# A streaming encoder layer: head norm's inverse root on one engine, the residual scaled before it is spilled, caches loaded earlier

## The chip, the cores and the metric

The kernel runs on one core of a Trainium2 chip. The core has a matrix engine (TensorE, PE in the profile, with PEld for its weight loads), a vector engine (VectorE, DVE), an activation engine (ScalarE, ACT), a general engine (GpSimd, POOL) and a queue that issues the transfers (SyncE, SP). Each engine works through its own instructions strictly in order; they wait for one another by semaphores. The metric is the device time of one execution in microseconds (us), the median of three runs.

## The reference

One layer of an encoder for 512 prompt tokens and 32 sample tokens, model width 1024. The mixer between two feed-forward halves holds what the change touches:

```
x = LN(ALPHA*x + 0.5*(1+g1)*SwiGLU1(mod1(x)))
z = mod2(x) @ w_in                       # retention q,k,v,gate | attention q,k,v | indexer
o_ret = head_norm(retention(rq, rk, rv)) * silu(rg)     # 4 heads of 128
o_att = attention over the top 128 keys (sample: 136) that the indexer admits   # 8 heads of 64
x = LN(ALPHA*x + (1+g2)*(concat(o_ret, o_att) @ w_out))
x = LN(ALPHA*x + 0.5*(1+g3)*SwiGLU2(mod3(x)))

def head_norm(x):                        # over the 128 columns of one head
    return (x - mean(x)) * rsqrt(var(x) + 1e-5)
```

## The kernel before

Activations lie transposed, 1024 rows as eight blocks of 128 partitions, and the 544 tokens as two halves of 272 columns. Every product is made of three float32r products (high by high, high by low, low by high), so a projection of one 128-column weight block and one half is 24 matmuls.

The order of PE is written out: `mm` and `turned` (lines 74 to 78) chain every matmul to the one before. Between the blocks of 24 matmuls of a projection, `tick` (line 93) lets side jobs run: generators that emit a few small products each and then yield a number of ticks. The order of DVE, ACT and POOL is set by a scheduler that lists instructions by priority and by its own estimates; a block under `tc.high_priority()` is preferred, and `tc.keep_in_program_order` pins an instruction. Transfers go through SP's queue in the order of `load`.

Around the change the program is this. After the first layer norm (`ln_to_h`, line 319) the normed input `h` is ready in halves, and the centred residual `xr` (four tiles of 128x1088) is spilled to memory without its factors (`spill`, line 768). The projections run in the order: four for the indexer, one more indexer query (line 766), then for each of four heads `retention` (line 806): q and k with rotary (`project_full`, line 595: ACT swaps halves into `sw`, DVE multiplies into `rqk`, POOL multiplies `sw` and adds), then v. Beside them run the side jobs: `indexer` (line 706) with score products `isc`, whose relus `rl` on ACT feed a running sum `wk` on DVE; `topk` (line 748), which takes the 128 largest scores in 16 rounds (17 for the sample) of max and match-replace on DVE; and each head's `side` (line 831): score products `rs`, their decay multiply `rsA`/`rsB` on DVE, output products `ro`, copied by ACT to `rsB`, `head_norm` (line 892) on it, the state product `rst`, copied to `Dm` (line 873), and the transposes `rot`.

`head_norm` takes mean and variance by `bn_stats`, then the inverse root: DVE makes a first exponent, ACT an Exp, DVE two Newton steps and the bias; ACT applies scale and bias to five pieces.

Then come the attention projections (`pair_inputs`), with `attention` (line 1006) as a side job: for each of 4 pairs of heads and 4 tiles the products `lg`, masks on DVE (`masked`, tile `mx`), softmax, transposes `pt` and values `po`. In the last stage, beside the gate projections (`gated`), `reload` (line 1067) fetches the residual as `xq` and multiplies it by the norm's factor on POOL and ACT (`residual_next`, line 346). `sample_attention` (line 959) does the 32 sample tokens, in two groups: products `sl`, transposes `spt`, values `spo`. Scores, `rs`, `rst`, `lg` and `sl` share two banks of tag "l".

```
def ordered(kind, r):
    if kind in last:
        tc.add_manual_dep(r.ins, last[kind], NOSYNC, reason="order of issue")
    last[kind] = r.ins.name
```

Of the kernel before, what the change touches and what calls it, by code (L numbers as in the profile page):

```python
# [16 lines left out]
P = 128  # L17
# [20 lines left out]
def encoder_layer_kernel(ctx, tc, xT, cT, wc1, w_cond, b_condT, lnp, w_gu1, w_dn1, w_in, w_out, w_gu2, w_dn2,  # L38
# [268 lines left out]
        nc.vector.scalar_tensor_tensor(y, v, 5.8 + 3.2 * q, y, op0=ALU.add, op1=ALU.mult)  # L307
        return y, centre

    def rsqrt(v, y, z):  # L310

        nc.vector.tensor_scalar(z, v.bitcast(I32), -2.0 ** -24, 0.5 * (127.0 - 0.043), op0=ALU.mult, op1=ALU.add)
        nc.scalar.activation(y, z, AF.Exp, scale=math.log(2.0))
        for f in (1.00017, 1.0):
            nc.vector.scalar_tensor_tensor(z, y, -0.5 * f, y, op0=ALU.mult, op1=ALU.mult)
            nc.vector.tensor_tensor(z, z, v, op=ALU.mult)
            nc.vector.scalar_tensor_tensor(y, z, 1.5 * f, y, op0=ALU.add, op1=ALU.mult)

    def ln_to_h(xr, G, B, name, first, gap):
        hn = []  # L320
        rs = [None, None]
# [21 lines left out]
                                                   op0=ALU.add, op1=ALU.subtract)  # L343
        return hn, rs, finish

    def residual_next(xr, rs, al, j):

        for i, (a, b) in enumerate(HALVES):
            rb = rs[i].unsqueeze(1).to_broadcast([P, 2, HT])
            tc.keep_in_program_order(nc.gpsimd.tensor_tensor(xr[j][:, :, a:b], xr[j][:, :, a:b], rb, op=ALU.mult))  # L350
        for d in (2 * j, 2 * j + 1):
            tc.keep_in_program_order(nc.scalar.activation(xv(xr, d), xv(xr, d), AF.Identity, bias=al[1][:, d:d + 1],
                                                          scale=al[0][:, d:d + 1]))
# [241 lines left out]
    def project_full(out):  # L595
        sw = scr("sw")

        def evac(ps, a, b):
            nc.scalar.copy(sw[0:64, a:b], ps[64:128])
            nc.scalar.copy(sw[64:128, a:b], ps[0:64])  # L600
            nc.vector.tensor_mul(out[:, a:b], ps, tabR[:, 0, a:b])  # L601

        project(evac)
        nc.gpsimd.tensor_mul(sw, sw, tabR[:, 1, :])  # L604
        nc.gpsimd.tensor_add(out, out, sw)
# [140 lines left out]
        flags.add(("score", 's'))  # L746

    def topk():
        for t, rate in ((1, 3), (2, 2), (3, 1), ('s', 1)):
            while ("score", t) not in flags:  # L750
                yield 1
            w = work[t]
            for n in range(17 if t == 's' else 16):
                m8 = sm.tile([P, 8], F32, name="m8", tag="m8")
                nc.vector.max(m8, w)  # L755
                nc.vector.match_replace(w, in_to_replace=m8, in_values=w, imm_value=MARK)  # L756
                if n % rate == rate - 1:
                    yield 1
            nc.vector.tensor_scalar(w, w, -3.3e38, NEG, op0=ALU.is_gt, op1=ALU.mult)
            if t != 's':  # L760
                L = P * (t + 1)
                nc.vector.memset(w[0:64, L - 64:L], NEG)
            flags.add(("mask", t))
# [4 lines left out]
    def spill():  # L768
        yield 0
        for j in range(4):  # L770
            nc.sync.dma_start(xd[j], xr[j].rearrange("p a t -> p (a t)"))

    spawn(spill())

# [31 lines left out]
    def retention(hh):  # L806
# [24 lines left out]
        def side():  # L831
# [26 lines left out]
            mm(po2[0:32, 0:P], qs, S0, start=False, stop=True)  # L858
            nc.scalar.copy(on, po)
            nc.scalar.copy(on2[0:32], po2[0:32, 0:P])  # L860
            head_norm([(on[:, n * P:(n + 1) * P], P) for n in range(4)] + [(on2[0:32], 32)])
            yield 1
            pk = bank("t", "rkt2")
            turned(pk[:, 0:P], k[:, 3 * P:TP], ident)
            turned(pk[0:32, P:2 * P], k[:, TP:T], ident)
# [26 lines left out]
    def head_norm(parts):  # L892
        n = len(parts)
        stt = sm.tile([P, n, 6], F32, name="bst", tag="bst")
        mv = sm.tile([P, n, 2], F32, name="bmv", tag="bmv")
        w = sm.tile([P, 3, n], F32, name="hnw", tag="hnw")
        nc.gpsimd.memset(mv[:, n - 1, :], 0.0)
        for j, (x, rows) in enumerate(parts):
            nc.vector.bn_stats(stt[:rows, j, :], x)
            nc.vector.bn_aggr(mv[:rows, j, :], stt[:rows, j, :])  # L900
        nc.vector.tensor_scalar(w[:, 0], mv[:, :, 1], EPS, None, op0=ALU.add)
        rsqrt(w[:, 0], w[:, 1], w[:, 2])
        nc.vector.scalar_tensor_tensor(w[:, 2], mv[:, :, 0], -1.0, w[:, 1], op0=ALU.mult, op1=ALU.mult)
        for j, (x, rows) in enumerate(parts):
            nc.scalar.activation(x, x, AF.Identity, bias=w[:rows, 2, j:j + 1], scale=w[:rows, 1, j:j + 1])


    def softmax_rows(Pt, mx):
# [48 lines left out]
        nc.vector.tensor_tensor(mixed[m][:, 1, a:b], src, mixed[m][:, 0, a:b].bitcast(F32), op=ALU.subtract)  # L957

    def sample_attention(g):
        yield from wait_for(("mask", 's'), ("pair", 2 * g + 1), ("att", 2 * g + 1))  # L960
        ck = unit("ck")
        load(ck[:, :, 0:512], ckT[2 * g:2 * g + 2].rearrange("c p t -> p c t"))
        cvt = up.tile([P, 4, 256], F32, name="cvt", tag="u")
        load(cvt, cv[g])
        yield 1
        ps, p2 = bank("l", "sl"), bank("l", "sl2")
        for j in range(4):
            c = 2 * g + j // 2
# [294 lines left out]
```

## Time and profile before

| what | value |
|---|---|
| median of three runs | 1255.4 us (1254.49 to 1256.1) |
| the profiled execution | 1258.19 us, of which the span from first to last instruction is 1256.4 us |
| PE busy | 1194.2 us (95%) |
| DVE busy | 810.7 us (65%) |
| POOL busy | 485.3 us (39%) |
| ACT busy | 435.2 us (35%) |
| mean granted TensorE clock | 0.977 of 2.4 GHz |

PE's busy time includes its time at a lower clock. The averages hide stages: between 520 and 650 us DVE is busy nearly all the time with the top-k rounds, while from 1000 us on it is busy a third of the time. A wait in the list of waits names the instruction that came last; which work stood in front of that instruction is read from the chain of waits and from the engine's timeline.

### The profile page before, as it was taken

To read this page: it belongs to the slowest core of one execution; us is meant where nothing else is said; L and a number is where in the kernel's file an instruction comes from. 1 tells how busy PE (TensorE), PEld (TensorE's weight loads), DVE (VectorE), ACT (ScalarE), POOL (GpSimd) and SP (SyncE) were. 2 spreads that over 40 slices of the span, in tenths; PEclk is the share of its full clock that TensorE was granted. 3 is DMA by queue.
4 is the path that set the end of the run, shared out by engine and by line. 5 is a ranking of instruction groups with operands and counts; after the bars stand their busy time and mean duration, and the time that the engine had idled before them with its cause. 6 is when DMAs were issued, how large, how long until landed. Compare 5 with 4: busy or idle time off the path is not lost.

```text
span 1256.4 us, 23057 instructions
## 1 busy us (share of the span) xinstructions
PE 1194.2 (95%) x9489; PEld 1145.9 (91%) x9489; DVE 810.7 (65%) x1469; ACT 435.2 (35%) x865; POOL 485.3 (39%) x244
## 2 busy tenths in 40 slices
PE   6999999999999989879999999999999999999995
PEld 4899999999989988767989887999999999999995
DVE  5786766865867585899985576797773333411616
ACT  2432322222113343442445555444422232221313
POOL 1554443443434334523433233332843334334420
PEclk9999999999999999988999998999999999999998
DMA  9554443434543142321233043420432322232212
GB/s 365 206 197 171 159 172 135 168 97 155 182 155 116 58 163 67 116 65 65 61 96 98 28 161 135 135 101 35 168 104 82 99 87 84 79 92 87 85 31 72
DMA packets 47562, 148.67 MB, mean 118 GB/s; under 512 B 6128, under 2 KB 9968, under 8 KB 47456
## 3 DMA queue, kind: packets, MB, share of 16 engines
q1 hardware_dynamic: 47456, 147.20, 34.3%
q8 instruction: 74, 1.21, 0.4%
q14 instruction: 32, 0.26, 0.1%
HBM read 138.05 MB, written 7.35 MB: 116 GB/s over the span
## 4 chain that ended last, share of the span: by engine, by line
PE 75%; DVE 13%; issue 4%; POOL 3%; DMA 2%; ACT 1%; SPq 0%; DVEq 0%; POOLq 0%; ACTq 0%
PE gu L75 39%; PE dn L75 18%; PE in L75 10%; PE gu_e L75 2%; POOL wh_w L132 2%; DVE wk L756 1%; DMA wc<-in_wc 1%; DVE m L755 1%; DVE wk L724 1%; PE lg L75 1%; PE pt L78 1%; PE po L75 1%; DVE xq L292 1%; PE cc L75 1%; DVE ht L339 1%
## 5 line engine op out<-in xcount | busy, mean ns | idle before, releaser
L132 POOL TENSOR_TENSOR wh_w<-wr_w,wh_w 128x1024 fp32r<-128x1024 f32 (+1 forms) x160 | 397.1, 2485 | 540.2 <-ACT wh_w L129 514.1
L75 PEld LDWEIGHTS gu<-h,wh_w 128*128 128x128 f32 x3840 | 481.5, 188 | 4.2 <-ACT tnh L183 2.5
L75 PE MATMUL gu<-h,wh_w 128*128 128x272 f32 x3840 | 483.6, 288 | 0.0
L75 PE MATMUL dn<-hid,wh_w 128*128 128x272 f32 x2112 | 267.1, 288 | 0.0
L75 PEld LDWEIGHTS dn<-hid,wh_w 128*128 128x128 f32 x2112 | 265.4, 188 | 1.0 <-issue 0.8
L129 ACT CAST wh_w<-wr_w 128x1024 fp32r<-128x1024 f32 (+1 forms) x162 | 165.8, 1026 | 176.6 <-PE dn L75 117.6
L75 PE MATMUL in<-h,wh_w 128*128 128x272 f32 x1392 | 196.7, 300 | 2.9 <-DVE rqk L601 2.9
L75 PEld LDWEIGHTS in<-h,wh_w 128*128 128x128 f32 x1392 | 185.2, 196 | 11.4 <-issue 5.9
L525 DVE SCALAR_TENSOR_TENSOR ca<-wc,cz,ca 128x1024 f32<-128x1024 f32 x98 | 182.6, 1889 | 14.9 <-DMA wc<-in_w_cond 14.9
L187 DVE TENSOR_TENSOR hid<-tnh,hid 128x272 fp32r<-128x272 f32 x88 | 87.2, 992 | 36.8 <-ACT hid L186 36.6
L185 DVE TENSOR_TENSOR tnh<-tnh,gu 128x272 f32<-128x272 f32 x81 | 35.3, 436 | 112.2 <-PE gu L75 112.2
L186 ACT CAST hid<-tnh 128x272 fp32r<-128x272 f32 x88 | 36.8, 419 | 141.6 <-DVE tnh L185 141.6
L183 ACT ACTIVATE tnh<-gu 128x272 f32<-128x272 f32 x80 | 31.5, 397 | 148.0 <-PE gu L75 148.0
L265 DVE SCALAR_TENSOR_TENSOR xq<-dn,C,xq 128x272 f32<-128x272 f32 (+2 forms) x48 | 17.9, 400 | 91.2 <-PE dn L75 91.2
L184 DVE SCALAR_TENSOR_TENSOR tnh<-tnh,gu 128x272 f32<-128x272 f32 x80 | 34.0, 430 | 54.3 <-ACT tnh L183 54.2
L755 DVE MAX8 m<-wk 128x8 f32<-128x544 f32 (+3 forms) x65 | 39.0, 600 | 1.2
L756 DVE MATCH_REPLACE8 wk<-m,wk 128x544 f32<-128x544 f32 (+3 forms) x65 | 38.0, 584 | 0.0
L604 POOL TENSOR_TENSOR sw<-sw,tabR 128x544 f32<-128x544 f32 x8 | 11.4, 1426 | 61.2 <-ACT sw L600 61.1
L132 POOL TENSOR_TENSOR wu_w<-wr_w,wu_w 128x1024 fp32r<-128x1024 f32 x8 | 19.8, 2474 | 36.7 <-ACT wu_w L129 30.9
L75 PE MATMUL in<-h,wu_w 128*128 128x272 f32 x192 | 26.5, 300 | 3.5 <-ACT h L341 2.9
L75 PEld LDWEIGHTS in<-h,wu_w 128*128 128x128 f32 x192 | 25.8, 199 | 4.0 <-ACT h L341 3.1
L75 PE MATMUL dn<-mx,wh_w 128*128 128x272 f32 x192 | 27.0, 301 | 0.0
(262 smaller groups left out, 1153.5 us busy)
## 6 DMA issues: line engine op xcount, KB each, us to landing
wr_w<-in_w_gu SPq DMA_DIRECT2D x84, 512.0 KB, 3.5
wc<-in_w_cond SPq DMA_DIRECT2D x56, 512.0 KB, 4.4
wr_w<-in_w_in SPq DMA_DIRECT2D x33, 512.0 KB, 4.0
wr_w<-in_w_dn SPq DMA_DIRECT2D x32, 448.0 KB, 3.3
wc<-in_wc SPq DMA_DIRECT2D x16, 512.0 KB, 10.6
wr_w<-in_w_dn SPq DMA_DIRECT2D x16, 512.0 KB, 3.5
wr_w<-in_w_out SPq DMA_DIRECT2D x8, 512.0 KB, 5.6
xr<-in_xT SPq DMA_DIRECT2D x4, 544.0 KB, 10.2
```

The source lines that it names most:

```text
L75: ordered("pe", nc.tensor.matmul(*a, **kw))
L129: c = nc.scalar.copy(hi[:, :n, :], raw[:, :n, :])
L132: (lo_eng or nc.gpsimd).tensor_tensor(lo[:, :n, :], raw[:, :n, :], hi[:, :n, :].bitcast(F32), op=ALU.subtract)
L183: nc.scalar.activation(t, pg, AF.Tanh, scale=0.5)
L184: nc.vector.scalar_tensor_tensor(t, t, 1.0, pg, op0=ALU.add, op1=ALU.mult)
L185: nc.vector.tensor_tensor(t, t, pu, op=ALU.mult)
L186: nc.scalar.copy(hid[:, 0, a:b], t)
L187: nc.vector.tensor_tensor(hid[:, 1, a:b], t, hid[:, 0, a:b].bitcast(F32), op=ALU.subtract)
L265: nc.vector.scalar_tensor_tensor(x[:, sa:sb], ps[:, sa - a:sb - a], coef[r][:, d:d + 1], x[:, sa:sb], op0=ALU.mult, op1=ALU.add)
L525: nc.vector.scalar_tensor_tensor(acc[r], w, c, acc[r], op0=ALU.mult, op1=ALU.add)
L755: nc.vector.max(m8, w)
L756: nc.vector.match_replace(w, in_to_replace=m8, in_values=w, imm_value=MARK)
```

## The change

Five edits. (1) The Exp of the head norm's inverse root goes: DVE starts from an integer guess and makes three Newton steps instead of two; the whole is under high priority, a small memset moves from POOL to DVE, and the five scalings on ACT are emitted one tick later. (2) The rotary multiply `rqk` gets high priority. (3) The residual is multiplied by the norm's factor (now on DVE) and scaled (on ACT) before the spill; `reload` only loads. The later call for the second norm stays on POOL. (4) The first top-k makes two rounds per tick instead of three. (5) `sample_attention` loads its caches as soon as its pair of heads is there, and waits for mask and attention afterwards, without a tick of its own in between.

```diff
-    def rsqrt(v, y, z):
-
-        nc.vector.tensor_scalar(z, v.bitcast(I32), -2.0 ** -24, 0.5 * (127.0 - 0.043), op0=ALU.mult, op1=ALU.add)
-        nc.scalar.activation(y, z, AF.Exp, scale=math.log(2.0))
-        for f in (1.00017, 1.0):
-            nc.vector.scalar_tensor_tensor(z, y, -0.5 * f, y, op0=ALU.mult, op1=ALU.mult)
-            nc.vector.tensor_tensor(z, z, v, op=ALU.mult)
-            nc.vector.scalar_tensor_tensor(y, z, 1.5 * f, y, op0=ALU.add, op1=ALU.mult)
...
-    def residual_next(xr, rs, al, j):
+    def residual_next(xr, rs, al, j, eng):
 
         for i, (a, b) in enumerate(HALVES):
             rb = rs[i].unsqueeze(1).to_broadcast([P, 2, HT])
-            tc.keep_in_program_order(nc.gpsimd.tensor_tensor(xr[j][:, :, a:b], xr[j][:, :, a:b], rb, op=ALU.mult))
+            tc.keep_in_program_order(eng.tensor_tensor(xr[j][:, :, a:b], xr[j][:, :, a:b], rb, op=ALU.mult))
...
-            nc.vector.tensor_mul(out[:, a:b], ps, tabR[:, 0, a:b])
+            with tc.high_priority():
+                nc.vector.tensor_mul(out[:, a:b], ps, tabR[:, 0, a:b])
...
-        for t, rate in ((1, 3), (2, 2), (3, 1), ('s', 1)):
+        for t, rate in ((1, 2), (2, 2), (3, 1), ('s', 1)):
...
         for j in range(4):
+            residual_next(xr, rs, al1, j, nc.vector)
             nc.sync.dma_start(xd[j], xr[j].rearrange("p a t -> p (a t)"))
+            yield 1
...
-            head_norm([(on[:, n * P:(n + 1) * P], P) for n in range(4)] + [(on2[0:32], 32)])
-            yield 1
+            normed = [(on[:, n * P:(n + 1) * P], P) for n in range(4)] + [(on2[0:32], 32)]
+            with tc.high_priority():
+                w = head_norm(normed)
+            yield 1
+            for j, (x, rows) in enumerate(normed):
+                nc.scalar.activation(x, x, AF.Identity, bias=w[:rows, 2, j:j + 1], scale=w[:rows, 1, j:j + 1])
...
-        nc.vector.tensor_scalar(w[:, 0], mv[:, :, 1], EPS, None, op0=ALU.add)
-        rsqrt(w[:, 0], w[:, 1], w[:, 2])
+
+        v, y, z = w[:, 0], w[:, 1], w[:, 2]
+        nc.vector.tensor_scalar(v, mv[:, :, 1], EPS, None, op0=ALU.add)
+        nc.vector.tensor_scalar(y.bitcast(I32), v.bitcast(I32), -0.5, float(0x5f3759df), op0=ALU.mult, op1=ALU.add)
+        for n in range(3):
+            nc.vector.scalar_tensor_tensor(z, y, -0.5, y, op0=ALU.mult, op1=ALU.mult)
+            nc.vector.tensor_tensor(z, z, v, op=ALU.mult)
+            nc.vector.scalar_tensor_tensor(y, z, 1.5, y, op0=ALU.add, op1=ALU.mult)
...
     def sample_attention(g):
-        yield from wait_for(("mask", 's'), ("pair", 2 * g + 1), ("att", 2 * g + 1))
+        yield from wait_for(("pair", 2 * g + 1))
         ck = unit("ck")
...
-        yield 1
+        yield from wait_for(("mask", 's'), ("att", 2 * g + 1))
...
-        yield 3
-        for j in range(4):
-            residual_next(xr, rs1, al1, j)
-            yield 1
```

What the scheduler makes of it, at three places. First DVE behind the last indexer query's rotary work (`rp`), before: the sum `wk` of the scores, the split `iqs` of that query and the decay multiplies `rsA` of the first head.

```order
L590 TENSOR_TENSOR rp<-rp 32x544
L601 TENSOR_TENSOR rqk<-in,tabR 128x272
L707 MEMSET wk_5139 128x128
L722 TENSOR_SCALAR wk_5138<-rl,ix 128x256
L708 MEMSET wk_5139 64x64
L724 SCALAR_TENSOR_TENSOR wk_5138<-rl,ix,wk_5138 128x256
L612 TENSOR_TENSOR iqs<-iqf,iqs 128x512
L724 SCALAR_TENSOR_TENSOR wk_5138<-rl,ix,wk_5138 128x256 x2
L839 TENSOR_TENSOR rsA<-rs,Dm 128x512
L839 TENSOR_TENSOR rsA<-rs,Dm 128x384
```

And in the changed kernel, where `xr` with a number is one of the four residual tiles.

```order
L581 TENSOR_TENSOR rp<-rp 32x544
L593 TENSOR_TENSOR rqk<-in,tabR 128x272
L699 MEMSET wk_5139 128x128
L714 TENSOR_SCALAR wk_5138<-rl,ix 128x256
L700 MEMSET wk_5139 64x64
L341 TENSOR_TENSOR xr_90<-xr_90,lny 128x2x272
L604 TENSOR_TENSOR iqs<-iqf,iqs 128x512
L341 TENSOR_TENSOR xr_89<-xr_89,lny 128x2x272 x2
L341 TENSOR_TENSOR xr_90<-xr_90,lny 128x2x272
L716 SCALAR_TENSOR_TENSOR wk_5138<-rl,ix,wk_5138 128x256
L341 TENSOR_TENSOR xr_91<-xr_91,lny 128x2x272 x2
L716 SCALAR_TENSOR_TENSOR wk_5138<-rl,ix,wk_5138 128x256
```

Six multiplies stand between the rotary add (`rp`) and the decay multiplies; the first two, of `xr_88`, stand ahead of the rotary work. On ACT the same place read thus before: casts, the relus `rl` that empty the score banks, the copy `vz`.

```order
L129 CAST wh_w<-wr_w 128x1024
L599 COPY sw<-in 64x272
L600 COPY sw<-in 64x272
L720 ACTIVATE rl<-isc 128x256 x2
L779 COPY vz<-in 128x272
L611 CAST iqs<-iqf 128x512
L720 ACTIVATE rl<-isc 128x256 x2
L779 COPY vz<-in 128x272
L129 CAST wh_w<-wr_w 128x1024
L720 ACTIVATE rl<-isc 128x256 x2
L129 CAST wh_w<-wr_w 128x1024 x2
```

And in the changed kernel.

```order
L129 CAST wh_w<-wr_w 128x1024
L343 ACTIVATE xr_88<-xr_88,ab_3321,ag_3320 128x544 x2
L590 COPY sw<-in 64x272
L591 COPY sw<-in 64x272
L712 ACTIVATE rl<-isc 128x256 x2
L773 COPY vz<-in 128x272
L603 CAST iqs<-iqf 128x512
L712 ACTIVATE rl<-isc 128x256
L773 COPY vz<-in 128x272
L343 ACTIVATE xr_89<-xr_89,ab_3321,ag_3320 128x544 x2
L129 CAST wh_w<-wr_w 128x1024
L343 ACTIVATE xr_90<-xr_90,ab_3321,ag_3320 128x544 x2
```

The scalings of a tile stand ahead of the swaps `sw` and the relus; those of the last two tiles and two weight casts stand ahead of the fourth relu. Second, DVE at the end of head 0's norm, before: `hnw` are the small operations of the inverse root, `m` and `wk` the top-k rounds.

```order
L756 MATCH_REPLACE wk_5138<-m_5891,wk_5138 128x256
L317 SCALAR_TENSOR_TENSOR hnw<-hnw 128x5
L755 MAX m_5894<-wk_5138 128x8
L315 SCALAR_TENSOR_TENSOR hnw<-hnw 128x5
L601 TENSOR_TENSOR rqk<-in,tabR 128x272
L316 TENSOR_TENSOR hnw<-hnw 128x5
L756 MATCH_REPLACE wk_5138<-m_5894,wk_5138 128x256
L317 SCALAR_TENSOR_TENSOR hnw<-hnw 128x5
L755 MAX m_5897<-wk_5138 128x8
L903 SCALAR_TENSOR_TENSOR hnw<-bmv,hnw 128x5
L756 MATCH_REPLACE wk_5138<-m_5897,wk_5138 128x256
```

And in the changed kernel, up to the last operation of the norm.

```order
L905 TENSOR_TENSOR hnw<-hnw 128x5
L747 MAX m_6041<-wk_5138 128x8
L906 SCALAR_TENSOR_TENSOR hnw<-hnw 128x5
L748 MATCH_REPLACE wk_5138<-m_6041,wk_5138 128x256
L904 SCALAR_TENSOR_TENSOR hnw<-hnw 128x5
L747 MAX m_6140<-wk_5138 128x8
L905 TENSOR_TENSOR hnw<-hnw 128x5
L716 SCALAR_TENSOR_TENSOR wk_5139<-rl,ix,wk_5139 128x384
L906 SCALAR_TENSOR_TENSOR hnw<-hnw 128x5
L748 MATCH_REPLACE wk_5138<-m_6140,wk_5138 128x256
L907 SCALAR_TENSOR_TENSOR hnw<-bmv,hnw 128x5
```

The last `hnw` operation has three Newton steps ahead of it and one more accumulate `wk<-rl` and more rounds in between. Third, PE at the sample attention, before: `sl` are its products, `dn` the output projection; the number after `sl` marks the group.

```order
L75 MATMUL sl<-ck,aV 32x512
L75 MATMUL sl_8710<-aV 32x32
L75 MATMUL dn_8742<-mx,wh_w 128x272 x24
L75 MATMUL sl<-ck,aV 32x512
L75 MATMUL sl_8769<-aV 32x32
L75 MATMUL sl<-ck,aV 32x512
```

And in the changed kernel.

```order
L75 MATMUL sl_8786<-aV 32x32
L75 MATMUL sl<-ck,aV 32x512
L75 MATMUL sl_8786<-aV 32x32
L75 MATMUL sl<-ck,aV 32x512
L75 MATMUL sl_8809<-aV 32x32
L75 MATMUL sl<-ck,aV 32x512
```

The 24 matmuls of the output projection between the two groups are gone from there; they stand ahead of both groups.

## Rows read from the trace of the kernel before

**Rows 1.** The page's first part: busy us, share of the span, instructions.
```profile
PE 1194.2 (95%) x9489; PEld 1145.9 (91%) x9489; DVE 810.7 (65%) x1469; ACT 435.2 (35%) x865; POOL 485.3 (39%) x244
```

**Rows 2.** Waits of PE from 480 to 860: waiter, releaser, us in total, times, longest.
```profile
PE isc L75 <- ACT Dm L873: 6.4, 1, 6.4
PE isc L75 <- DVE rsA L839: 4.6, 2, 3.6
PE lg L75 <- DVE mx L918: 4.3, 4, 2.2
PE in L75 <- DVE rqk L601: 2.9, 1, 2.9
PE sl L75 <- issue: 2.9, 1, 2.9
PE rot L78 <- ACT rsB L905: 0.9, 1, 0.9
PE isg L75 <- ACT Dm L873: 0.5, 1, 0.5
```

**Rows 3.** Windows: stretch, length, busy us by engine, granted clock, DMA share, GB/s.
```profile
540.00:550.00 10.00, 7.39 (x32) 6.55 (x33) 8.70 (x27) 3.81 (x11) 0.00 (x0) 0.56 0.45 134
750.00:760.00 10.00, 7.03 (x32) 6.11 (x31) 8.96 (x15) 3.74 (x11) 10.00 (x7) 0.68 0.00 0
760.00:770.00 10.00, 8.69 (x53) 6.79 (x52) 7.88 (x26) 7.25 (x18) 2.72 (x2) 0.80 0.38 133
780.00:790.00 10.00, 7.13 (x65) 6.17 (x58) 6.47 (x18) 5.40 (x7) 3.55 (x2) 0.89 0.49 159
```

**Rows 4.** Chain of waits from 485 to 560: start us, us, what.
```profile
537.74 1.97 DVE hnw L903
540.13 0.99 ACT rsB L905 x3
542.61 1.33 PE isc L75 x6
543.94 5.44 PE in L75 x24
551.99 3.19 PE in L75 x24
```

**Rows 5.** Timeline of PE: start, us, operation, count, idle before and releaser.
```profile
505.27 0.62 PE L75 MATMUL isc<-iks,iqs 64*128 64x256 f32 x6 [0.94 <-DVE rsA L839]
513.70 0.62 PE L75 MATMUL isc<-iks,iqs 64*128 64x256 f32 x6 [3.64 <-DVE rsA L839]
```

**Rows 6.** Timeline of DVE from 470 to 516.
```profile
496.50 2.80 DVE L590 TENSOR_TENSOR rp<-rp 32x544 f32<-32x544 f32 x1
508.54 4.90 DVE L724 SCALAR_TENSOR_TENSOR wk<-rl,ix,wk 128x256 f32<-128x256 f32 x2 [2.86 <-ACT rl L720]
```

**Rows 7.** Timeline of ACT from 470 to 516.
```profile
502.28 0.62 ACT L611 CAST iqs<-iqf 128x512 fp32r<-128x512 f32 x1
507.17 1.05 ACT L129 CAST wh_w<-wr_w 128x1024 fp32r<-128x1024 f32 x1 [3.44 <-DMA wr_w<-in_w_in]
```

**Rows 8.** Timeline of DVE from 514 to 560: the first top-k selection.
```profile
517.17 0.43 DVE L755 MAX8 m<-wk 128x8 f32<-128x256 f32 x1
```

**Rows 9.** Four source lines: ns min/median/max, first and last start us, forms.
```profile
L222 DVE TENSOR_TENSOR xr<-xr,shc x8: 710/714/715, 375.8 to 382.8; 128x544 f32<-128x544 f32 x8
L350 POOL TENSOR_TENSOR xq<-xq,lny x16: 1346/1466/2347, 748.2 to 888.4; 128x544 f32<-128x544 f32 x16
L352 ACT ACTIVATE xq<-xq,ab,ag x16: 825/834/845, 753.8 to 890.5; 128x544 f32<-128x544 f32 x16
L903 DVE SCALAR_TENSOR_TENSOR hnw<-bmv,hnw x4: 155/1096/2212, 537.7 to 650.4; 128x5 f32<-128x5 f32 x4
```

**Rows 10.** The page's costliest groups: busy us, mean ns of one, idle before.
```profile
L755 DVE MAX8 m<-wk 128x8 f32<-128x544 f32 (+3 forms) x65 | 39.0, 600 | 1.2
L756 DVE MATCH_REPLACE8 wk<-m,wk 128x544 f32<-128x544 f32 (+3 forms) x65 | 38.0, 584 | 0.0
```

More of the change, by code (lines that the diff above doesn't have):

```diff
@@ L896, in head_norm @@
         w = sm.tile([P, 3, n], F32, name="hnw", tag="hnw")
-        nc.gpsimd.memset(mv[:, n - 1, :], 0.0)
+        nc.vector.memset(mv[:, n - 1, :], 0.0)
         for j, (x, rows) in enumerate(parts):
@@ L900, in head_norm @@
             nc.vector.bn_aggr(mv[:rows, j, :], stt[:rows, j, :])
-        nc.vector.tensor_scalar(w[:, 0], mv[:, :, 1], EPS, None, op0=ALU.add)
-        rsqrt(w[:, 0], w[:, 1], w[:, 2])
+        v, y, z = w[:, 0], w[:, 1], w[:, 2]
[5 more added lines that the diff above has]
+            nc.vector.scalar_tensor_tensor(y, z, 1.5, y, op0=ALU.add, op1=ALU.mult)
         nc.vector.scalar_tensor_tensor(w[:, 2], mv[:, :, 0], -1.0, w[:, 1], op0=ALU.mult, op1=ALU.mult)
-        for j, (x, rows) in enumerate(parts):
-            nc.scalar.activation(x, x, AF.Identity, bias=w[:rows, 2, j:j + 1], scale=w[:rows, 1, j:j + 1])
+        return w
     def softmax_rows(Pt, mx):
@@ L1069, in reload @@
             load(xr[j].rearrange("p a t -> p (a t)"), xd[j])
-        yield 3
-        for j in range(4):
-            residual_next(xr, rs1, al1, j)
-            yield 1
-    rs1 = rs
     for hh in range(4):
@@ L1079, in encoder_layer_kernel @@
             xr = [unit(f"xq{j}") for j in range(4)]
-            spawn(reload())
+            reload()
         assert ("ret", hh) in flags
@@ L1112, in residual @@
         for j in range(4):
-            residual_next(xr, rs, al2, j)
+            residual_next(xr, rs, al2, j, nc.gpsimd)
             yield 1
```

## The prediction

> **What bounds the kernel now.** I read five views, in this order. The page's first part: TensorE (PE) is busy 1194.2 of 1256.4 us [rows 1], so waits and a lowered clock are all that a change off TensorE can win or lose. The list of PE's waits between 480 and 860 us, the stretch that the change touches: 22.5 us in the seven that bear on it, led by a 6.4 us wait for the copy of the retention state, 4.6 us for the decay multiplies `rsA` of VectorE (DVE), 4.3 us for the masks `mx`, 2.9 us for the rotary multiply `rqk`, and 2.9 us put down to "issue" [rows 2]. The windows: the granted clock falls behind the larger of these waits, to 0.56, 0.68, 0.80 and 0.89 of 2.4 GHz, thus to its 1.2 GHz level for part of each stretch [rows 3]. The chain of waits around 540 us, which says whose work is late [rows 4]. Last the timelines of the engines where the change puts new work [rows 5 to 8]. The reader is to see that PE's order is written out by hand, so that each PE wait has one late instruction on DVE or ScalarE (ACT), and that these two run strictly in order.
>
> **Term 1, residual multiplied on DVE ahead of the spill: +9.4 us.** Eight multiplies of 128x544 (0.71 us each when nothing is in the way) go to DVE, and eight scalings (0.83 us each) to ACT, both into 490 to 515 us [rows 9]. Two of the multiplies now stand ahead of the last index query's rotary work. There DVE already has to wait for GpSimd (POOL): the rotary add took 2.80 us where its like takes 0.71 [rows 6, 9], 2.1 of it waiting. The two multiplies are 1.42 us, and I add 1.3 us for one more meeting with POOL: the add ends at 502.0 instead of 499.3 us (bounds 500.7 with no meeting, 503 with two). Its result goes through a DMA to ACT, whose cast began at 502.28, 3.0 us after the add [rows 6, 7]: now 505.0. From there everything is one chain, because the order puts it in front of the relu that empties the bank of the third score group: cast 0.62, split 0.7, two multiplies 1.42, two scalings 1.67, a weight cast 1.05, four scalings 3.34, a weight cast 1.05 [rows 7, 9], 9.85 us in all, to 514.9. The third group started at 505.27 [rows 5], so PE is 9.6 us late there. That is some 10 us of waiting in two pieces, the first already at the second score group, whose bank waits for a relu that ACT now gives behind the first scalings. After the 6.4 us wait of rows 2 a block of 24 matmuls took 5.44 us and later 3.19 [rows 4]; I charge the same 2.25 us for the clock. In return most of the wait of 3.6 us before the fourth group (4.6 in two waits [rows 2]) goes, as its DVE work is no longer late: I keep 1.1 of it and win 2.5. 9.6 + 2.25 - 2.5 = 9.4. Lower bound: add at 500.7, third group 8.3 late, no clock loss, wait gone whole: 8.3 - 3.6 = 4.7. Upper: 11, with a third meeting with POOL. DVE's top-k selections start 3.5 us behind the fourth group (517.17 against 513.70 [rows 5, 8]) and DVE has few gaps after that (8.7 us busy of 10 in the window from 540 us [rows 3]), so nothing gives this back before 600 us.
>
> The spill's four DMAs (128 x 1088 floats each) move there too and stand in SP's queue behind the scalings and ahead of the second batch of weights. I cost them at nothing, because that batch serves the projections of the next head, not those at hand. If the cover goes, the price is like the 3.44 us that ACT waited for weights at 507 us [rows 7].
>
> **Term 2, head norm: +4.6 us.** It removes one Exp on ACT per head and adds three small DVE operations. The chain around 540 us contains no Exp: the late link is DVE's last `hnw` operation, then ACT's `rsB`, then the copy that PE waits for [rows 4]. So the removal wins nothing by itself. What decides is where DVE's order puts the chain, and the order shows it mixed with more selections than before: up to head 0's last operation two match-replaces and one max more, and one accumulate of the index score that stood behind it. At about 0.5 us for each of the three narrow selections (0.60 and 0.58 are the means over all widths [rows 10]), 0.3 for the accumulate's share and 3 x 0.155 for the new operations [rows 9], head 0's copy is 2.2 us later. Head 1: two match-replaces, a max and a compare more, 1.9, and 0.5 for the new operations: 2.4. There PE waits 0.5 us for that copy already [rows 2], so it is paid in full. Heads 2 and 3 have one wait of 0.9 us between them [rows 2]; I take 0. Bounds: each of these operations has two SBUF operands and takes 0.155 us alone and up to 2.21 beside POOL [rows 9]; one meeting fewer or more in each head is -2 or +2 each: from 0 to +9.
>
> **Term 3, attention's last stage: -7.3 us.** The same eight multiplies leave POOL and ACT between 748 and 772 us, where one takes 1.47 us on POOL and 0.71 on DVE [rows 9]. PE waits 4.3 us for masks there [rows 2], and the clock costs 10 x 0.32 x 0.70 + 10 x 0.20 x 0.87 = 4.0 us (loss of clock times busy share in two windows [rows 3]): 8.3 at most. I keep 1 us: in the new DVE order one of the two masks of the last head pair's second tile stands behind a gate product that needs the next projection. Bounds -8.3 and -3.
> What the Trainium skill says on this ("Perfetto Trace Analysis", section "Optimizing Scalar/DVE Operations") is that moving work between GpSimd and VectorE may not help, since the two share a read port of SBUF. By that rule term 3 is 0 and the sum +11.8 instead of +4.5. The rows agree that the two get in each other's way, but the work also leaves the stage, so I hold with the rows here; term 1 is the rule's case.
>
> **Term 4, sample attention: -2.2 us.** Both halves now issue their products in one tick, and DVE has its mask ready earlier: the 2.9 us wait and 10 x 0.11 x 0.71 = 0.8 us of clock go [rows 2, 3]. Three places come in their stead where one bank is emptied between back-to-back groups (second product, second transpose, the mean): about 0.5 us each, an estimate, 1.5 in all. Bounds -3.7 and +1.
>
> **At nothing:** the memset on DVE stands at the start, beside the first weight loads. The cache loads were no wait of PE before [rows 2]; hidden by three attention tiles. The rotary multiply at high priority: the order still has two splits of the queries ahead of the first one, so its 2.9 us wait stays (bound -2.9). The slower pace of the first selection puts the fourth attention tile three half projections later; the gaps in which attention waited for the next pair take that up, and if they don't, one more block of 3.2 us [rows 4] comes at the end.
>
> **Sum.** 9.4 + 4.6 - 7.3 - 2.2 = +4.5 us. The profiled execution took 1258.2 us, 2.8 above the median of the three timed runs, so I put the sum on that median: 1255.4 + 4.5 = 1259.9, say 1260.
>
> **Rivals.**
> *Faster: the multiplies fit in between.* If DVE runs all eight while POOL is idle and the clock stays at 2.4 GHz, term 1 is its lower bound 4.7 and the head norms cost nothing because their chain starts earlier: 4.7 - 7.3 - 2.2 = -4.8, 1250.6 us. For it: DVE has 2.9 us of idle time in that stretch, waiting for a relu [rows 6]. Against it: that relu is on ACT, which is the engine that fills up. It decides if the third score group starts before 510 us.
> *No change: the head norms are free.* Terms 1, 3 and 4 cancel: -0.1, 1255.3 us. For it: PE reaches head 0 later, so DVE may be less behind. Against it: DVE's own start moves by as much.
> *Much slower: the masks stay late.* The gate products keep standing in front of the masks, term 3 is 0: +11.8, 1267 us. For it: each gate has three DVE operations in every tick of the last stage. Against it: POOL is the releaser's neighbour in that stage alone. The rule of the Trainium skill weighed under term 3 would come out here.
>
> **How the numbers follow.** Forecast 0.45, much slower 0.10, no change 0.22, faster 0.23. The forecast's own range is 1258 to 1264. A measurement of this kernel can tell 0.2% (2.5 us) from no change. So faster 0.23, within 0.22, slower 0.55. Range: the faster rival with a better term 4 (1248) to the much slower one (1268); about 0.08 is left out on each side.
>
> **What would show it.** Right: the third score group (`isc` of 256 columns) starts near 515 us, behind a wait of over 5 us released by ACT; between 500 and 550 us the clock is lower than before; the wait for the state copy (`Dm`) grows to about 8 us and at head 1 to about 3; waits for `mx` fall below 2 us; the first wait for `rqk` is still 2.9. Wrong: term 1 if that group starts before 511 us; term 2 if the time from the first `bn_stats` to the last `hnw` operation of head 0 is below 10 us; term 3 if PE still waits over 3 us for `mx`; term 4 if the waits around `sl`, `spt` and `shp` sum to more than 3.5 us. The whole is wrong if 650 us's work starts less than 8 us later than now.

## The result, and the profile after

The changed kernel takes 1271.8 us (median of 4 runs, 1271.1 to 1274.3) where the kernel before takes 1255.2: ratio 1.0136, 95% interval 1.0118 to 1.0153, 16.7 us slower. I forecast 1260 and a range up to 1268: the sign was right, the size too small by 12 us. The profiled execution took 1271.9 us with a span of 1270.1, 13.7 us above the span before. In a later comparison (e5 to e8) two of eighteen executions of the kernel before took 1918 us at a granted clock of 0.56; the ratios leave them out.

TensorE's waits between 480 and 860 us, which answer to [rows 2]:

```profile
PE isc L75 <- DVE Dm L875: 8.1, 1, 8.1
PE spt L78 <- ACT Psu L991: 5.8, 1, 5.8
PE isg L75 <- DVE Dm L875: 4.3, 1, 4.3
PE rot L78 <- ACT rsB L860: 4.1, 1, 4.1
PE in L75 <- DVE rqk L593: 3.8, 1, 3.8
PE isc L75 <- DVE rsA L833: 3.8, 1, 3.8
PE isc L75 <- ACT rl L712: 3.1, 2, 2.8
```

The 4.3 us for `mx` of the last attention tiles and the 2.9 us "issue" before `sl` are gone. In their place stand a new wait at the sample's second transpose (`spt`, 5.8), and longer ones at every head norm that TensorE waits for: `Dm` of head 0 from 6.4 to 8.1, `Dm` of head 1 from 0.5 to 4.3, `rot` of head 3 from 0.9 to 4.1.

To see which stage pays, I cut the span at work that is in every kernel, by the time at which TensorE starts it: the index weights' transposes (`piw`), the first value product of head 0 and of head 3 (`ro`), the first score product of the attention (`lg`), the first output product (`dn`), the second feed-forward (`gu_e`). These times are read from TensorE's timeline; the columns are the us between them.

| kernel | to `piw` | S1: to `ro`, head 0 | S2: heads 0 to 2 | S3: head 3, to `lg` | S4: attention, to `dn` | S5: output and sample, to `gu_e` | rest | span |
|---|---|---|---|---|---|---|---|---|
| before | 476.4 | 47.1 | 109.8 | 26.4 | 115.5 | 64.2 | 416.9 | 1256.4 |
| before, again (e5) | 475.1 | 46.8 | 109.3 | 26.4 | 115.7 | 65.6 | 417.1 | 1255.9 |
| changed | 476.4 | 53.4 | 113.4 | 32.1 | 109.1 | 68.6 | 417.2 | 1270.1 |
| e1 norm undone | 474.7 | 53.3 | 110.5 | 26.4 | 110.8 | 68.4 | 416.9 | 1260.9 |
| e2 residual undone | 477.7 | 45.1 | 112.8 | 32.1 | 115.0 | 68.5 | 416.7 | 1267.9 |
| e3 cache late | 476.3 | 53.9 | 113.9 | 32.2 | 107.8 | 68.8 | 417.3 | 1270.3 |
| e4 fast selection | 475.2 | 53.2 | 113.4 | 32.1 | 111.5 | 59.5 | 417.2 | 1262.2 |
| e6 norm held together | 476.5 | 53.9 | 94.6 | 24.3 | 115.3 | 68.6 | 417.2 | 1250.4 |
| e7 before + early residual | 475.4 | 45.7 | 111.5 | 26.4 | 107.6 | 64.1 | 416.8 | 1247.5 |
| e8 three mends on before | 476.5 | 43.8 | 98.5 | 24.3 | 121.3 | 61.5 | 417.2 | 1243.2 |
| e9 two Newton steps | 476.4 | 53.3 | 110.4 | 25.9 | 108.6 | 68.1 | 417.2 | 1260.0 |
| e10 `rqk` priority undone | 476.5 | 54.2 | 113.2 | 30.7 | 108.8 | 67.8 | 417.2 | 1268.5 |
| e11 three mends on changed | 475.2 | 43.9 | 98.5 | 24.3 | 121.2 | 61.2 | 417.3 | 1241.5 |
| e12 before + slow selection | 474.7 | 46.5 | 109.3 | 26.4 | 116.1 | 68.0 | 416.9 | 1257.9 |

Changed minus before: S1 +6.3, S2 +3.6, S3 +5.7, S4 -6.4, S5 +4.4. The rest is the same within 0.3, so nothing is given back later. The two profiles of before differ by 1.4 us in S5 (64.2 and 65.6), so a difference of that size in S5 says nothing; in the other stages they agree within 0.5.

In S1 the third score group came where I had forecast it. TensorE there, beside [rows 5] (start, duration, then in brackets the wait and its releaser):

```profile
505.68 1.67 PE L75 MATMUL rs<-rqk 128*128 128x512 f32 x4
511.14 0.58 PE L75 MATMUL isc<-iks,iqs 64*128 64x256 f32 x1 [3.79 <-DVE rsA L833]
514.53 1.00 PE L75 MATMUL isc<-iks,iqs 64*128 64x256 f32 x5 [2.82 <-ACT rl L712]
```

and ScalarE (ACT) ahead of it, where the relu `rl` that frees the bank stands behind the residual's scalings (L343):

```profile
507.82 1.57 ACT L343 ACTIVATE xr<-xr,ab,ag 128x544 f32<-128x544 f32 x2 [1.47 <-DVE xr L341]
509.30 1.03 ACT L129 CAST wh_w<-wr_w 128x1024 fp32r<-128x1024 f32 x1
510.24 3.03 ACT L343 ACTIVATE xr<-xr,ab,ag 128x544 f32<-128x544 f32 x4
513.17 1.03 ACT L129 CAST wh_w<-wr_w 128x1024 fp32r<-128x1024 f32 x1
514.11 0.37 ACT L712 ACTIVATE rl<-isc 128x256 f32<-128x256 f32 x1
```

The two multiplies ahead of the rotary work, and the rotary add itself, on VectorE (DVE):

```profile
494.20 4.68 DVE L341 TENSOR_TENSOR xr<-xr,lny 128x544 f32<-128x544 f32 x2
500.93 0.71 DVE L581 TENSOR_TENSOR rp<-rp 32x544 f32<-32x544 f32 x1
```

S3 is what I had at nothing. Head 3's norm on DVE, part of its timeline:

```profile
648.76 0.47 DVE L897 BATCH_NORM_STATS2 bst<-rsB 128x6 f32<-128x128 f32 x2
...
650.81 0.71 DVE L748 MATCH_REPLACE8 wk<-m,wk 128x544 f32<-128x544 f32 x1
651.44 2.25 DVE L901 TENSOR_SCALAR hnw<-bmv 128x5 f32<-128x5 f32 x1
653.60 0.71 DVE L747 MAX8 m<-wk 128x8 f32<-128x544 f32 x1
654.23 0.14 DVE L902 TENSOR_SCALAR hnw<-hnw 128x5 int32<-128x5 int32 x1
...
657.59 0.71 DVE L748 MATCH_REPLACE8 wk<-m,wk 128x544 f32<-128x544 f32 x1
658.22 0.15 DVE L905 TENSOR_TENSOR hnw<-hnw 128x5 f32<-128x5 f32 x1
658.30 0.77 DVE L579 STREAM_SHUFFLE rp<-rp 64x544 f32<-64x544 f32 x1
658.96 1.98 DVE L906 SCALAR_TENSOR_TENSOR hnw<-hnw 128x5 f32<-128x5 f32 x1
...
663.48 0.14 DVE L907 SCALAR_TENSOR_TENSOR hnw<-bmv,hnw 128x5 f32<-128x5 f32 x1
```

Between two steps of 0.15 us on five columns stands a max or a match-replace of 0.71 us on 544. From the first `bn_stats` (648.76) to the last `hnw` (663.62) head 3 takes 14.9 us, before 10.3; heads 0 to 2 take 11.2, 12.8 and 13.1, before 10.0, 10.5 and 11.4. The two steps of 2 us meet POOL, whose `wh_w` subtractions run at 651.29 and 658.54. In the kernel before, the norm of head 3 met one such subtraction, and late in it; its only long step was

```profile
642.93 1.03 DVE L901 TENSOR_SCALAR hnw<-bmv 128x5 f32<-128x5 f32 x1
```

So of the 4.6 us by which head 3's norm grew, some 3 are meetings with POOL (2.25 and 1.98 us in place of 1.03 and 0.15). The rest is one more selection (8 in place of 7), a rotary add of 0.71 us that now stands ahead of the last step, and the three new steps. In heads 0 to 2 the steps lose no more to POOL than before. TensorE's block after the wait for `rot` shows the granted clock at 0.73 from 660 to 670 us (5.66 us for 24 matmuls, later 3.24), while 750 to 790 is at full speed: it holds the work of 750 to 770 in [rows 3], which TensorE now reaches 9 to 15 us later:

```profile
660.00:670.00 10.00, 5.80 (x23) 4.80 (x23) 5.00 (x11) 4.14 (x10) 1.83 (x5) 0.73 0.38 119
750.00:760.00 10.00, 9.80 (x82) 8.21 (x81) 7.45 (x18) 6.51 (x14) 4.91 (x2) 1.00 0.27 77
760.00:770.00 10.00, 9.98 (x90) 8.37 (x89) 7.27 (x28) 7.17 (x20) 0.00 (x0) 1.00 0.59 212
780.00:790.00 10.00, 10.00 (x94) 9.36 (x93) 6.83 (x11) 6.50 (x14) 4.12 (x2) 1.00 0.13 41
```

### The profile page after: what moved, and what is told of

The parts are those of the page before. It is cut to its first block, busy times and chain, and to the rows that moved or that the text cites. A ratio compares the mean times of both kernels' runs of the same rounds, so it can differ in the third digit from the quotient of the medians.

```text
span 1270.1 us, 23050 instructions
## 1 busy us (share of the span) xinstructions
PE 1193.4 (94%) x9489; PEld 1144.2 (90%) x9489; DVE 812.3 (64%) x1493; ACT 435.6 (34%) x861; POOL 473.6 (37%) x232
## 4 chain that ended last, share of the span: by engine, by line
PE 72%; DVE 15%; issue 4%; DMA 3%; ACT 2%; POOL 2%; SPq 1%; DVEq 0%; POOLq 0%; ACTq 0%
PE gu L75 38%; PE dn L75 17%; PE in L75 9%; PE gu_e L75 2%; DVE wk L748 2%; DVE m L747 2%; POOL wh_w L132 1%; DMA wc<-in_wc 1%; DVE wk L716 1%; PE lg L75 1%; PE pt L78 1%; PE po L75 1%; DVE xq L292 1%; DVE hnw L906 1%; PE cc L75 1%
## 5 line engine op out<-in xcount | busy, mean ns | idle before, releaser
L184 DVE SCALAR_TENSOR_TENSOR tnh<-tnh,gu 128x272 f32<-128x272 f32 x80 | 34.1, 430 | 54.4 <-ACT tnh L183 54.2
L75 PE MATMUL isc<-iks,iqs 64*128 64x256 f32 (+2 forms) x72 | 11.4, 402 | 15.8 <-DVE Dm L875 8.1
```

Of the source, the lines that this page charges most:

```text
L75: ordered("pe", nc.tensor.matmul(*a, **kw))
L184: nc.vector.scalar_tensor_tensor(t, t, 1.0, pg, op0=ALU.add, op1=ALU.mult)
```

## The experiments

My theory A: each part's price is the stage in the table, and the head norm is late because selections stand between its steps. Each experiment takes one part away, puts one in alone, or removes the cause that A names.

### e1 to e4: one part of the change undone

e1, the norm as before (`rsqrt` with Exp, two steps, scalings behind it):

```
...
-            with tc.high_priority():
-                w = head_norm(normed)
...
+            head_norm([(on[:, n * P:(n + 1) * P], P) for n in range(4)] + [(on2[0:32], 32)])
...
+        rsqrt(w[:, 0], w[:, 1], w[:, 2])
```


> The changed kernel with the head norm as before (seed by Exp on ScalarE, two Newton steps, no priority, scaling right behind it). Theory A (the third Newton step and the selection pairs between its steps make each head's copy late: head 0 +1.5, head 1 +2.0, head 3 +5.7 with its slow clock): 1262 to 1264 us, and TensorE's wait for rot falls from 4.1 to under 1.5. Rival B (head 3's lateness comes from the slower first selection beside it): the wait for rot stays over 3 and the time over 1268.

1264.6 us, ratio 1.0080 (1.0065 to 1.0095): 7.0 us of the 17 come from the norm. S2 and S3 are back (110.5, 26.4), the wait for `rot` is 0.9. Theory A holds, with the time 0.6 us above its range; rival B falls, since the slow selection was still there. Head 3's norm is back at 10.3 us, with one step of 1.02 us beside POOL, so this run takes away the added meetings together with the added steps.

e2, the residual on POOL after its reload:

```
-            residual_next(xr, rs, al1, j, nc.vector)
...
+            residual_next(xr, rs1, al1, j, nc.gpsimd)
```


> The changed kernel with the residual as before (POOL and ScalarE, after its reload). Theory A (its two ends, +6.2 at 490 to 522 and -7.6 in the last attention stage, nearly cancel): 1271 to 1274 us, waits for mx of 4 us come back at the last attention tiles and the first retention value product starts 5 to 6 us earlier. Rival C (the residual part alone makes the kernel slower): 1266 or less.

1267.4 us, 1.0109 (1.0094 to 1.0124): the part costs some 3.4 us net by the ratios and 2.4 by S1 and S4, more than theory A had (about nothing), less than rival C. S1 falls by 8.3, to 2.0 less than before, and S4 rises by 5.9. The waits for `mx` are 0.4 only; `po` waits 3.2 for ScalarE instead, so S4's price is there, but behind another instruction.

e3, the cache loaded as before, behind the mask:

```
-        yield from wait_for(("pair", 2 * g + 1))
+        yield from wait_for(("mask", 's'), ("pair", 2 * g + 1), ("att", 2 * g + 1))
...
-        yield from wait_for(("mask", 's'), ("att", 2 * g + 1))
+        yield 1
```


> The changed kernel with the sample's cache loaded late, as before. Theory A (the 4.3 us lost in the sample's attention come from the slower first selection, which moves group 0 next to group 1): 1270 to 1274 us, the second spt still waits over 4 us. Rival D (the early load took the tick between the groups): the wait goes and the time is 1267 to 1268.

1272.3 us, 1.0151 (1.0134 to 1.0168), not told apart from the changed kernel; S5 stays 68.8. Rival D falls.

e4, three selection pairs per half-projection for the first score tile:

```
-        for t, rate in ((1, 2), (2, 2), (3, 1), ('s', 1)):
+        for t, rate in ((1, 3), (2, 2), (3, 1), ('s', 1)):
```


> The changed kernel with three selection pairs per half-projection for the first score tile, as before. Theory A: the groups of the sample's attention come apart again, its 4.3 us go, and the two waits for aV (2.0) too: 1265 to 1268 us. Rival D (early load): 1270 or more with the second spt waiting over 4. Rival B also has rot's wait at head 3 fall under 1.5 us here: then 1260 to 1263.

1264.9 us, 1.0088 (1.0073 to 1.0103): 6 us from this one number. S5 falls from 68.6 to 59.5, below the 64.2 before; part of it returns in S4 (+2.4, with a wait of 2.2 for `mx`). Rival B falls again: `rot` still waits 4.1. The trace of the changed kernel shows why two neighbouring groups cost so much. TensorE:

```profile
803.98 0.71 PE L78 MATMUL spt<-cm,Psu 128*128 128x128 f32 x5
810.46 1.33 PE L78 MATMUL spt<-cm,Psu 128*128 128x128 f32 x5 [5.77 <-ACT Psu L991]
```

ScalarE, which has to empty the bank of the first transposes for the second:

```profile
805.43 1.04 ACT L129 CAST wu_w<-wr_w 128x1024 fp32r<-128x1024 f32 x1
809.50 0.42 ACT L214 CAST shr<-S 128x272 fp32r<-128x272 f32 x1 [3.03 <-DVE S L212]
809.83 0.58 ACT L991 COPY Psu<-spt 128x512 f32<-128x512 f32 x1
```

The copy (L991) could have run at 806.5. It stands in order behind the mean's cast (L214), which waits for a sum `S` on DVE, and that sum started at 806.89 and took 2.58 us beside three POOL subtractions (7.39 us from 801.77).

### e5 and e12: the kernel before, and with the slow selection alone

> The kernel before once more, unchanged, for a second profile. The profiled execution of before took 1258.2 us, its timed runs 1254 to 1255. Theory A1: the 3 to 4 us more lie in the first 470 us, which the change doesn't touch, and the four waits for mx (4.3) with the slow clock behind them return here. Rival: they lie in those waits, that is, other executions have fewer of them and the residual's end of the ledger (-7.6) was an exception of one profile: then the last attention stage is 3 us shorter here.

1257.7 us in its profiled execution, stages as in the first profile, 5.6 us of waits for `mx`: S4's gain is no accident of one profile. The rival falls, and so does A1: the first 470 us are the same within 1.3, and why the profiled executions of before are 2 to 3 us above its timed runs no stage shows.

> The kernel before with one edit, two selection pairs per half-projection for the first score tile in place of three. Theory A (that edit alone moves group 0 of the sample's attention next to group 1): from the first output product to the second feed-forward takes 68 to 70 us in place of 64.2, with a wait of over 4 for the second spt, and the time is 1257 to 1261 us beside 1254 to 1255. Rival: it costs only in company with the late head norms: that stretch stays under 66 and the time within 2 us of before.

```
-        for t, rate in ((1, 3), (2, 2), (3, 1), ('s', 1)):
+        for t, rate in ((1, 2), (2, 2), (3, 1), ('s', 1)):
```

On the kernel before: 1260.2 us, 1.0048 (1.0029 to 1.0067): S5 is 68.0 and `spt` waits 5.3 (two waits, the longer 4.6). This part costs its 6 us alone (3.6 to 8.4 by the interval).

### e6 and e9: the selections between the norm's steps

e6 is the changed kernel with one edge: a max written after a head norm goes behind the norm's last instruction (`held[0]`) on DVE.

```
-                nc.vector.max(m8, w)
+                r = nc.vector.max(m8, w)
+                if held[0]:
+                    tc.add_manual_dep(r.ins, held[0], NOSYNC, reason="behind the head norm")
```


> The changed kernel, with one ordering edge more: a selection pair that is written later than a head norm goes behind its last instruction, so that the norm's 22 instructions stand together on VectorE. Theory A (the pairs between its steps make the norm late): first bn_stats to last hnw of head 0 falls from 11.2 to 4 to 6 us, the waits for Dm (8.1 and 4.3) and rot (4.1) fall under 3 in sum, and the time is 1252 to 1259 us. Rival E (what is late is the scaling on ScalarE, or POOL's lock hits the steps all the same): waits of over 8 in sum stay and the time is over 1264.

1251.5 us, ratio 0.9974 (0.9964 to 0.9985) to the kernel before: the changed kernel, 1.4% slower without this edge, is faster with it, and a little below theory A's range. Heads 0 to 3 take 4.9, 6.4, 4.1 and 3.9 us. S2 is 18.8 us shorter than in the changed kernel and S3 7.8; S4 takes 6.2 back. The end of head 3's norm, to be read against its rows in the changed kernel above:

```profile
631.15 0.16 DVE L907 SCALAR_TENSOR_TENSOR hnw<-hnw 128x5 f32<-128x5 f32 x1
631.35 0.17 DVE L908 TENSOR_TENSOR hnw<-hnw 128x5 f32<-128x5 f32 x1
631.55 0.17 DVE L909 SCALAR_TENSOR_TENSOR hnw<-hnw 128x5 f32<-128x5 f32 x1
631.75 0.17 DVE L910 SCALAR_TENSOR_TENSOR hnw<-bmv,hnw 128x5 f32<-128x5 f32 x1
631.83 0.69 DVE L747 MAX8 m<-wk 128x8 f32<-128x512 f32 x1
```

A dependent step follows every 0.20 us, and a norm this short meets POOL in one long step only (1.36 us, head 1). So the edge removes the selections and nearly all meetings at once. TensorE's waits for `Dm` are 0.3 and 0.2, for `rot` none.

e9 is the changed kernel with

```
-        for n in range(3):
+        for n in range(2):
```


> The changed kernel with two Newton steps in place of three (the root is coarser, some 5e-6 of it). Theory A (each step's three instructions stand behind a selection pair or its like each): head 3's norm falls from 14.9 to 10 to 11 us and its wait for rot from 4.1 to under 1, the waits for Dm from 8.1 and 4.3 to 6 to 7 and under 2: 1262 to 1265 us. Rival E (POOL's lock or the scaling sets it): the norms get shorter by under 1 us each and the time stays over 1268.

1260.8 us, 1.0051 (1.0036 to 1.0066): the third Newton step, three instructions of 0.15 us in each head, costs 0.85%, some 10.7 us. Heads take 9.7, 11.1, 11.6 and 9.9 us, so 1.5 to 1.7 us less in heads 0 to 2 and 5.0 in head 3. Of the 5.0, some 3 are again the meetings: head 3 has one long step of 1.01 us here, and POOL's next subtraction comes 3.4 us after the norm's end. That it missed the norm is a matter of timing, so the 11 us are not the price of a step as such. Its long step, and its waits (changed: 8.1, 4.3, 4.1):

```profile
649.70 1.01 DVE L901 TENSOR_SCALAR hnw<-bmv 128x5 f32<-128x5 f32 x1
```

```profile
PE isc L75 <- ACT Dm L871: 6.9, 1, 6.9
PE isg L75 <- ACT Dm L871: 1.1, 1, 1.1
PE rot L78 <- ACT rsB L860: 0.4, 1, 0.4
```

### e7: the residual where DVE is idle

On the kernel before; all of the residual's lines after the reload go, and behind the second normalisation stands

```
+    for j in range(4):
+        residual_next(xr, rs, al1, j, nc.vector)
     rope_turn(rp, (z, 1), *((q, 2) for q in qs[:3]))
```


> The kernel before with the residual's multiplications on VectorE and its scalings on ScalarE as in the change, but written right behind the second normalisation (VectorE is idle there for 8.3 us from 468.6), and none after the reload; all else as before. Theory A (the residual's loss is the place, its gain the last attention stage): the stage from 490 to 522 is as in before, and the waits for mx go: 1245 to 1249 us beside before. Rival F (the gain at the end was owed to the later selections): the waits for mx stay and the time is that of before within 2 us.

1251.5 us, 0.9971 (0.9957 to 0.9986). S1 is 45.7 (before 47.1) and S4 107.6 (before 115.5), with 0.7 us of waits for `mx`. The trace shows both gains, 1.4 and 7.9, and a loss of 1.7 in S2; the timed runs give 3.6 us (1.8 to 5.4), less than the 6 to 9 of theory A. Of the difference, 2 to 3 us are what before's profiled executions lie above its timed runs, and 2.2 what e7's lies below its own median. Rival F falls: the waits for `mx` go without the slower selection. The eight multiplies:

```profile
467.49 5.17 DVE L350 TENSOR_TENSOR xr<-xr,lny 128x544 f32<-128x544 f32 x8
475.90 0.19 DVE L672 TENSOR_SCALAR ix<-piw 128x32 f32<-128x32 f32 x1 [3.24 <-PE piw L78]
```

### e10: the priority of `rqk` undone

```
-            with tc.high_priority():
-                nc.vector.tensor_mul(out[:, a:b], ps, tabR[:, 0, a:b])
+            nc.vector.tensor_mul(out[:, a:b], ps, tabR[:, 0, a:b])
```


> The changed kernel without the high priority of the retention queries' and keys' product on VectorE. Theory A (the wait for rqk before 493 ends with the rope table's load, not with VectorE's order): the wait of 3.8 stays within 0.6 and the time within 3 us of 1272. Rival H (the priority costs, since the third product goes ahead of the residual and the index queries): 1266 to 1268.

1270.9 us, 1.0132 (1.0115 to 1.0149); the wait for `rqk` is 3.8 as with it. The priority buys and costs nothing that can be measured. Nor can the norm's priority matter: written without it, the program has the same order on every engine, but for a memset at the start of DVE. No run was made of that.

### e8 and e11: what the mends give together

e8 is before with e7's edit, the norm of the change held as in e6 (no priority), and the early cache; e11 the changed kernel with the edits of e4, e6 and e7.

> The kernel before with three edits: the residual behind the second normalisation as in e7, the head norm's root by three Newton steps on VectorE with no selection pair between its steps (scaling right behind it, no priority), and the sample's cache loaded early. Theory A: e7's -6 to -9, and head 0's wait of 6.4 with the slow clock behind it (3.4) and head 3's 0.9 go, the sample's wait of 2.9 too: 1234 to 1241 us. Rival E: the waits for Dm stay over 5: 1244 to 1249.

> The changed kernel with three mends: selection pairs behind the norm as in e6, the residual written behind the second normalisation as in e7, three selection pairs per half-projection for the first score tile as in e4. Theory A by the ledgers (-20 for the held norm, -8 for the place, -6.7 for the selection, less what VectorE can't give: it was 97% busy from 650 to 700 in e8): 1237 to 1243 us, VectorE again over 95% busy in the first attention tiles. Rival: the selections aren't the bound, and the three add up: 1230 to 1236.

e8: 1241.4 us, 0.9892 (0.9874 to 0.9911). e11: 1239.9 us, 0.9887 (0.9870 to 0.9905). Both beat both kernels, and the parts don't add up: S2 and S3 give 13.4 us against before, but S4 is 121 us where e7 has 107.6. Added up over the stages, TensorE starts the output projection at 764.6 us in e6, 766.6 in e7, 764.4 in e8 and 763.1 in e11 (before: 775.2): the held norm and the moved residual together reach that point hardly sooner than either alone, and what e8 and e11 are ahead of e6 and e7 is S5. In e11 DVE, which does the selections, has hardly a break from 640 us on (third busy column; the last but two is the clock):

```profile
670.00:680.00 10.00, 9.79 (x85) 8.97 (x85) 10.00 (x40) 5.08 (x13) 0.87 (x1) 1.00 0.46 164
680.00:690.00 10.00, 4.90 (x44) 4.12 (x40) 10.00 (x12) 3.86 (x10) 8.28 (x7) 0.85 0.33 103
690.00:700.00 10.00, 9.24 (x61) 7.14 (x61) 7.38 (x27) 7.04 (x18) 1.32 (x1) 0.81 0.09 29
```

and in the middle one only 12 instructions long. Three of them:

```profile
679.90 2.75 DVE L580 TENSOR_TENSOR rp<-rp,tabA 64x1088 f32<-64x1088 f32 x1
682.70 2.79 DVE L581 TENSOR_TENSOR rp<-rp 64x544 f32<-64x544 f32 x1
685.41 2.42 DVE L921 TENSOR_SCALAR Pu<-Pu,rl 128x256 f32<-128x256 f32 x1
```

They take 1.27, 0.71 and 0.35 us elsewhere. POOL subtracts weights meanwhile:

```profile
679.13 2.37 POOL L132 TENSOR_TENSOR wh_w<-wr_w,wh_w 128x1024 fp32r<-128x1024 f32 x1 [19.22 <-ACT wh_w L129]
681.69 6.00 POOL L132 TENSOR_TENSOR wh_w<-wr_w,wh_w 128x1024 fp32r<-128x1024 f32 x2 [0.19 <-ACT wh_w L129]
```

TensorE waits 5.1 us for a `mx` of L963 just there. By this reading S4's loss is a busy DVE that three meetings with POOL push over. That moving these subtractions would win it back was not tried.

## Why the prediction was wrong

**Term 2, head norm: heads 0 to 2 right, head 3 the first step that failed.** S2 cost 3.6 us (I had 4.6), with `Dm` of head 0 at 8.1 (I had 8) and of head 1 at 4.3 (I had 3; e5 shows that wait at 1.7 in the kernel before, so it varies by over 1 us). "Heads 2 and 3 have one wait of 0.9 us between them; I take 0" was wrong for head 3: S3 cost 5.7, 3.3 of it more wait for `rot` and 2.4 the slow clock. I took the small present wait for slack, when it meant that there was none: TensorE arrives there just as the scaling is done, so of a norm 4.6 us longer 3.3 are paid as wait. And I gave head 3 no longer norm at all, although my own bounds had one more meeting with POOL at 2 us a head: some 3 of the 4.6 us are such meetings, the rest one selection of 0.71 us, a rotary add and the new steps. e1, e9 and e6 show that with fewer steps, or none of them between selections, the waits go. In heads 0 to 2 the meetings are as long with the third step as without, and S2 falls by 3 us (e1, e9): there the steps and their neighbours are the cause. In head 3 all three runs take meetings away too, and how much of its loss would be left with the meetings held fixed no run shows. That the removal of the Exp wins nothing by itself is borne out: e9 without it has S2 and S3 within 0.6 us of e1, which has it.

**Term 4 and an edit "at nothing": the second step that failed.** I had "both halves now issue their products in one tick" down as a gain of 2.2 from the early cache. That the groups meet comes from the slower first selection (e4, e12), not from the cache (e3), and it is a loss (S5 +4.4, or +3.0 against e5): `sl`, `spt` and `shp` sum to 8.5 us of waits against my bound of 3.5. I priced each bank that a neighbouring group must wait for at 0.5 us, by the time that emptying it takes, and not by what stands ahead of that on ScalarE. With the groups apart the early cache does win what I had given it: S5 is 61.5 in e8 and 61.2 in e11 beside e7's 64.1. The slower selection, which I costed at nothing or 3.2 us, costs some 6.

**Term 1: mechanism right, +6.3 and not +9.4.** The five matmuls of the third group start at 514.53 (I had 514.9). The way there was in part luck: the rotary add ends at 501.64 where I had 502.0, but the meetings fell on the two multiplies (4.68 us, which I had at 1.42), and the add, which I gave 2.8 us and one meeting more, met POOL not at all (0.71). The slow clock behind the third group cost 1.4 us and not 2.25. What I had too small is what comes back: the wait before the fourth group fell by 2.9, from 3.64 to 0.69 (I had 2.5), and the block behind it runs at full clock, 3.26 us where it took 4.81 before. By e2 the residual alone costs S1 8.3, nearer my 9.4; the rest of the change gives 2.0 back there, and by which edit no run shows. e7 shows the loss to be of the place, of multiplies and scalings together. Two of the signs that I had named for this term didn't show: the wait came in two pieces, 3.79 us released by `rsA` on DVE and 2.82 by ScalarE, and the clock from 500 to 550 us was not lower than before (0.88 and 0.86).

**Term 3: right, -6.4 and not -7.3.** No wait for `mx` of the attention's tiles is left, and the clock from 750 to 790 is 1.00. The rival that the masks stay late is refuted, although its 1267 lies near the result. The rule weighed there (the Trainium skill, "Perfetto Trace Analysis", "Optimizing Scalar/DVE Operations": moving work between POOL and DVE may not help) is borne out by the net where DVE was busy (e2: a loss of some 3 us) and not where it was idle (e7: 0.3% faster). Term 3 itself, to which I had applied it, goes against it in both.

**At nothing:** cache loads and `rqk`'s priority rightly so (e3, e10), and the spill's transfers too: from 495 to 560 us ScalarE has no wait for weights in the changed kernel (3.8 us before). The memset was not run alone.

Sum of the misses: head 3 +5.7, sample +6.6, heads 0 to 2 -1.0, term 1 -3.1, term 3 +0.9, together 9.1 of the 12 us. The other 3 are the distance of before's profiled executions from the median of its timed runs (e5), which the changed kernel's profile doesn't have. They lie within the spread of the timed runs (1252.9 to 1258.4 in e5's comparison); why stays open.

## What to carry to other kernels

A chain of tiny dependent instructions on a shared in-order engine costs what stands between its links, and what its links run into meanwhile, not its own time: count the neighbours and the meetings, and tie the chain together before making it shorter or longer (here one ordering edge was worth 20 us, and a Newton step 11, some of it chance). A wait that is nearly zero is not slack; ask how early the waited-for work was done, and charge every delay beyond that. Where a pace moves, look for groups that become neighbours and share a bank, and price the bank by the queue ahead of its reader.

## What the runs showed of the hardware

VectorE needs 0.20 us from one dependent step on 128x5 to the next, each 0.16 to 0.17 us long (e6): the scheduler had put other work into gaps that hardly exist. The same kinds of step took 1.98 and 2.25 us where POOL ran a subtraction of 2.4 us on 128x1024. The Trainium skill ("SBUF — State Buffer", section "Who interferes with whom") calls the port that the two share an exclusive lock; these rows agree, as do the three of e11, and with several POOL operations in a row the wait recurs for each one on VectorE. The selections are not held up: in the changed kernel these three ran while POOL subtracted from 640.75 for 2.39 us.

```profile
640.81 0.73 DVE L747 MAX8 m<-wk 128x8 f32<-128x544 f32 x1
641.65 0.71 DVE L748 MATCH_REPLACE8 wk<-m,wk 128x544 f32<-128x544 f32 x1
642.39 0.73 DVE L747 MAX8 m<-wk 128x8 f32<-128x544 f32 x1
```
